# A second mixture in 11 column tiles: the third tile in strips that a count gives out, its weights copied by ScalarE, and a ring of 13 wide tiles in the first mixture

## The chip, the core and the metric

The kernel runs on one core of a Trainium2 chip. TensorE is called PE here, VectorE DVE, ScalarE ACT, GpSimd POOL and SyncE SP. The metric is the device time of one launch in microseconds (us): 2194.33 us, the median of three runs (2190.61 to 2199.8). The execution that the profiler recorded took 2192.68 us.

## The reference, cut to what matters

Two transformer blocks run one after the other on 256 tokens of 1024 features, in float32. Both have a mixture of experts; all else (attention, time mixing, dense products, norms) is not touched by the change but for a few places of buffers.

```python
def expert_block(args):              # first mixture: 32 experts, hidden 512, two experts for a token
    xb, e = args
    return (jax.nn.silu(xb @ w_gate[e]) * (xb @ w_up[e])) @ w_down[e]
...
def moe_swiglu(x, router_w, router_b, w1, w3, w2):   # second mixture: 8 experts, hidden 2816
    logits = (x @ router_w + router_b).astype(jnp.float32)
    top_v, top_i = lax.top_k(logits, TOP_K)          # TOP_K = 2
    top_p = jax.nn.softmax(top_v, axis=-1)
    gate = jnp.sum(jax.nn.one_hot(top_i, N_EXPERTS_2, dtype=jnp.float32) * top_p[..., None], axis=-2)
    out = jnp.zeros_like(x)
    for e in range(N_EXPERTS_2):
        out = out + gate[..., e:e + 1] * swiglu(x, w1[e], w3[e], w2[e])
    return out
```

With 256 tokens and two experts for each, an expert of the first mixture gets 16 tokens in the mean, one of the second 64. With the inputs of the runs no expert of the first mixture has more than 30; those of the second have 81, 47, 76, 46 and 65, 81, 65, 51.

## The kernel before

The program is a list of phases, run in order: `b1` (first block's mixer), `moe1` (first mixture), `mix0`, `ffn0`, `ple0`, `mix1`, `ffn1` (the second mixture, function `moe2`), `ple1`, `fin`. Weights come from memory as tiles of 1 MB (128x2048) that SP loads, in the order in which they are used, into a ring of places; a load is issued as soon as the tile that had its place before is released. A phase can widen the ring: `WIDE` gives the number of places that it adds, 9 in `moe1` (12 with the three of the base) and 6 in `ffn1`.

A mixture routes tokens by matrix products. A one-hot matrix `P` (tokens by slots) is made on DVE from the place of each token in its expert's list (`At`, `places`, `pos`); PE gathers the tokens of the slots with it (`gathered`, into `xg`); the experts' products are computed for slots; and the results are combined back with the transposed and weighted matrix (`pw`, `pt`). If an expert has more tokens than slots, a branch (`overflow`, an If on all engines, on the flag `fi` that DVE makes) computes the rest; with these inputs the branch's body is not run, but its test is.

**First mixture.** 32 experts with 32 slots each, 8 groups `g` of four experts. A group takes 16 tiles `wgu` (first products) and 8 tiles `wdn` (down). The test of the overflow stands after group 3.

**Second mixture.** The 8 experts are two halves `c` of four. For each half there are 11 blocks `j` of first products, each of 8 tiles `w<-m` (`k`, a slice of 128 of the 1024 features; four experts side by side, 512 columns each), then two down products `d` of 22 tiles each: 264 tiles in all. Each expert has `CAP2` = 96 slots, so that a half has 384 slots, which are three PSUM banks of 128. The function `tiles` does one tile: 12 matmuls, each of 32 slots (the stationary side) by 512 columns of the slots' expert, each on a quarter (32 columns) of the array. Four quarters make one bank, so a tile is three rounds of four.

After the 8 tiles of a block `j`, ACT does Silu on each bank's gate half (`ft`, 128x256) and DVE multiplies by the other half; DVE transposes the result in pieces into `hT`, the input of the down product. At the end of a down product (below called a d-end) ACT takes each bank with a scale to `yh` (128x512), DVE takes what rounding left to `yl`, and PE combines both into the tokens with `pt`. The banks are double: the next block can use three others meanwhile. The overflow's test stands at `c` = 1, `j` = 5. In `route_in` the input is split in a high and a low part (`htmh`, `html`); of four low parts two are made on DVE and two on POOL.

Instructions go to each engine's queue in program order, but for work put in `beside` or `later`, which is laid between the tiles. All queues run in order.

Of the kernel before, what the change touches and what calls it, by code (L numbers as in the profile page):

```python
# [119 lines left out]
def prep(I):  # L120
# [88 lines left out]
    g, u = [I[n][0].reshape(2, 4, 8, 128, 11, 256).transpose(0, 4, 2, 3, 1, 5) for n in ("moe_w1_2", "moe_w3_2")]  # L209
    A["m13"] = np.concatenate([g, u], -1)  # L210
# [65 lines left out]
class Kern:  # L276
# [275 lines left out]
    def run(self):  # L552
        tc, nc, A = self.tc, self.nc, self.A
        with ExitStack() as ctx:
# [4 lines left out]
            self.wsp = pool("wsp", SPLIT)  # L559
# [27 lines left out]
            self.room, wider = ExitStack(), set()  # L587
# [6 lines left out]
            for i, ph in enumerate(self.phases):  # L594
                l = int(ph[-1]) if ph[-1].isdigit() else 0
                if ph == "ple0":
                    other = split(second.enter_context(tc.tile_pool(reuse_waits="tile", name="raw", bufs=1)))
                new = (self.phases + [""])[i + 1]
                self.ends = new == "fin"
# [18 lines left out]
                if ph == "mix1":  # L618
                    second.close()
            if self.phases[-1] != "fin":  # L620
                nc.sync.dma_start(self.out.rearrange("k p s -> p k s"), x)
# [16 lines left out]
    def block1(self, x, early):  # L638

        tc, nc = self.tc, self.nc  # L640
        with ExitStack() as late, ExitStack() as ctx:
# [6 lines left out]
            nc.gpsimd.dma_start(a2, self.A["a2"])  # L648
            h = [pool.tile([128, 8, S], F32R, name="h" + c) for c in "hl"]
# [41 lines left out]
            out = late.enter_context(tc.tile_pool(reuse_waits="tile", name="b1o", bufs=1, side="right"))  # L691
            mg = out.tile([128, 8, S], F32, name="mg")
            mh = out.tile([128, 8, S], F32R, name="mh")
            ml = out.tile([128, 8, S], F32R, name="ml")
# [231 lines left out]
    def places(self, pool, oh1, oh2, n, beside):  # L926
# [6 lines left out]
        for t in range(2):  # L933
            o = b.t[:, n * t:n * t + n]
            b.mm(o, self.cst("triu"), At[:, t])
            if t:
                b.mm(o, self.cst("ones"), At[:, 0])
        with self.after((nc.cur_bb, added)):
# [3 lines left out]
        nc.vector.scalar_tensor_tensor(ps, pv, 1.0, At, op0=ALU.add, op1=ALU.mult)  # L942
        return ps
# [19 lines left out]
    def overflow(self, pool, x, xs, rs, wo, fi, n, units, w13, w2):  # L963
# [3 lines left out]
        tc, nc = self.tc, self.nc  # L967
        wT = pool.tile([32, S], F32, name="wT")
        ec = pool.tile([32, 2], F32, name="ec")
        rv = nc.values_load(fi, min_val=0, max_val=1, skip_runtime_bounds_check_because="made by a comparison")  # L970
        with tc.If(rv != 0, preferred_fallthrough_block=False):  # L971
# [10 lines left out]
            for k in range(8):  # L982
                nc.vector.tensor_mul(xs[:, k], xs[:, k], b.t[:, :S])
# [4 lines left out]
            def unit(i, e):  # L988
                nc.vector.scalar_tensor_tensor(ec[:, 1:2], ec[:, 0:1], float(e), self.cst("pidx")[:32],
                                               op0=ALU.add, op1=ALU.is_equal)  # L990
                sel = self.wsp.tile([128, 512], F32, name="wh")
# [1068 lines left out]
```

## Time and the profile before

| | |
|---|---|
| time, median of three runs | 2194.33 us (2190.61 to 2199.8) |
| profiled execution | 2192.68 us, of which the recorded span is 2191.1 us |
| PE busy | 2047.4 us, 93% of the span |
| DVE, ACT, POOL busy | 48%, 29%, 1% |
| memory traffic | 613.44 MB, 280 GB/s in the mean |
| first mixture, its products | about 345 to 800 us |
| second mixture, its products | about 1420 to 2142 us |

The span is cut into stages by the tiles that are loaded. A busy share of a whole span says little here: in one stretch PE waits for loads, in another loads wait for PE. So the stages are read apart, by what stood in the windows and by which engine's wait ends last.

### The profile page before, as it was taken

To read this page: it belongs to the slowest core of one execution; us is meant where nothing else is said; L and a number is where in the kernel's file an instruction comes from. 1 tells how busy PE (TensorE), PEld (TensorE's weight loads), DVE (VectorE), ACT (ScalarE), POOL (GpSimd) and SP (SyncE) were. 2 spreads that over 40 slices of the span, in tenths; PEclk is the share of its full clock that TensorE was granted. 3 is DMA by queue.
4 is the path that set the end of the run, shared out by engine and by line. 5 is a ranking of instruction groups with operands and counts; after the bars stand their busy time and mean duration, and the time that the engine had idled before them with its cause. 6 is when DMAs were issued, how large, how long until landed. Compare 5 with 4: busy or idle time off the path is not lost. (4 is left out here: it accounts for less than half of the span.)

```text
span 2191.1 us, 39956 instructions
## 1 busy us (share of the span) xinstructions
PE 2047.4 (93%) x16640; PEld 1241.8 (57%) x16640; DVE 1061.6 (48%) x2770; ACT 629.9 (29%) x1298; POOL 23.7 (1%) x33
## 2 busy tenths in 40 slices
PE   7999998787787779999999999999999999999997
PEld 6999995222222238889999988842222333233336
DVE  5787654010000028677666777636554006555105
ACT  5466642000000025365556735410000000001005
POOL 0000000000000010000000100000000000000000
PEclk9999999999999999999999999899999999999999
DMA  5344586999999983315555341479999999999972
GB/s 177 118 145 138 174 343 260 420 419 420 418 420 420 420 363 117 119 59 200 190 192 189 113 138 40 173 264 384 410 407 409 388 377 402 400 363 408 409 306 91
DMA packets 88640, 613.44 MB, mean 280 GB/s; under 512 B 9879, under 2 KB 12071, under 8 KB 18560
## 3 DMA queue, kind: packets, MB, share of 16 engines
q1 hardware_dynamic: 86272, 604.74, 70.8%
q0 software_dynamic: 1344, 5.10, 0.7%
q8 instruction: 133, 2.18, 0.4%
q10 hardware_dynamic: 832, 0.94, 0.1%
q14 instruction: 59, 0.48, 0.1%
HBM read 609.69 MB, written 1.05 MB: 279 GB/s over the span
## 5 line engine op out<-in xcount | busy, mean ns | idle before, releaser
L228 PE MATMUL ps<-w,xg 128*32 128x512 f32 x2432 | 428.9, 600 | 54.9 <-DMA w<-wgu 48.2
L340 DVE TENSOR_TENSOR wl<-w,wh 128x512 fp32r<-128x512 f32 (+2 forms) x500 | 318.9, 652 | 169.4 <-ACT wh L339 158.5
L339 ACT CAST wh<-w 128x512 fp32r<-128x512 f32 (+2 forms) x500 | 289.6, 585 | 296.1 <-PE ps L228 254.6
L228 PE MATMUL ps<-w,hT 128*32 128x512 f32 x2624 | 338.3, 593 | 30.3 <-DMA w<-wdn 24.9
L228 PEld LDWEIGHTS ps<-w,xg 128*32 128x32 f32 x2432 | 97.9, 110 | 306.0 <-issue 180.7
L228 PE MATMUL ps<-rawh,wh 128*128 128x256 f32 x896 | 258.9, 289 | 0.0
L1989 DVE STREAM_TRANSPOSE hT<-ft 32x64 f32<-32x64 f32 x1056 | 249.2, 236 | 17.7 <-DVEq L971 0.7
L228 PE MATMUL ps<-rawh,wl 128*128 128x256 f32 x896 | 252.5, 282 | 1.5 <-DVE rawl L353 1.5
L228 PE MATMUL ps<-rawl,wh 128*128 128x256 f32 x896 | 252.3, 282 | 0.0
L228 PEld LDWEIGHTS ps<-w,hT 128*32 128x32 f32 x2624 | 91.2, 110 | 264.6 <-issue 189.7
L228 PE MATMUL ps<-w,rawl 128*32 128x512 f32 x1408 | 201.9, 597 | 5.2 <-DVE hT L1989 5.2
L228 PEld LDWEIGHTS ps<-rawh,wh 128*128 128x128 f32 x896 | 169.6, 189 | 3.8 <-issue 1.4
L228 PEld LDWEIGHTS ps<-rawh,wl 128*128 128x128 f32 x896 | 169.7, 189 | 3.5 <-DVE rawl L353 1.7
L228 PEld LDWEIGHTS ps<-rawl,wh 128*128 128x128 f32 x896 | 169.5, 189 | 1.1 <-DVE ast L1789 0.2
L228 PE MATMUL ps<-w,rawh 128*32 128x512 f32 x1408 | 167.9, 595 | 0.0
L301 ACT ACTIVATE ft<-ps,rsl 128x256 f32<-128x256 f32 x66 | 31.3, 474 | 415.8 <-PE ps L228 415.8
L228 PE MATMUL ps<-hh,wh 128*128 128x256 f32 x416 | 125.8, 303 | 0.0
L228 PEld LDWEIGHTS ps<-w,rawl 128*32 128x32 f32 x1408 | 56.5, 111 | 110.7 <-issue 108.9
L228 PE MATMUL ps<-hh,wl 128*128 128x256 f32 x416 | 117.4, 284 | 0.1
L228 PE MATMUL ps<-hl,wh 128*128 128x256 f32 x416 | 117.3, 282 | 0.0
L1981 DVE SCALAR_TENSOR_TENSOR ft<-ps,rsl,ft 128x256 f32<-128x256 f32 x66 | 31.9, 484 | 168.5 <-ACT ft L301 167.1
L1204 DVE SCALAR_TENSOR_TENSOR sg<-ps,rsl,sg 128x512 f32<-128x512 f32 x8 | 6.0, 749 | 209.1 <-PE ps L228 175.8
(492 smaller groups left out, 2708.8 us busy)
## 6 DMA issues: line engine op xcount, KB each, us to landing
w<-m SPq DMA_DIRECT2D x264, 1024.0 KB, 7.3
w<-wgu SPq DMA_DIRECT2D x128, 1024.0 KB, 19.9
w<-wdn SPq DMA_DIRECT2D x64, 1024.0 KB, 19.9
w<-f SPq DMA_DIRECT2D x32, 1024.0 KB, 4.9
w<-wz SPq DMA_DIRECT2D x20, 1024.0 KB, 5.0
w<-wdh SPq DMA_DIRECT2D x24, 768.0 KB, 4.3
w<-wb SPq DMA_DIRECT2D x16, 1024.0 KB, 5.1
w<-wo SPq DMA_DIRECT2D x8, 1024.0 KB, 5.3
```

What stands on the lines that cost most here:

```text
L228: return self.k.nc.tensor.matmul(out, lhsT, rhs, start=new, stop=stop, skip_group_check=True, **kw)
L301: r = sc.activation(out, in_, func, **kw)
L339: self.nc.scalar.copy(h, src)
L340: self.nc.vector.tensor_sub(l, src, h.bitcast(F32))
L1204: nc.vector.scalar_tensor_tensor(sg, acc[1].t, rsl[:, g:g + 1], sg, op0=ALU.mult, op1=ALU.mult)
L1981: nc.vector.scalar_tensor_tensor(t, g[r].t[:, 256:], u, t, op0=ALU.mult, op1=ALU.mult)
L1989: nc.vector.transpose(hT[f:f + 32, 2 * j:2 * j + 2, 128 * r + s:128 * r + s + 32], ts[r].rearrange("p (i d) -> p i d", i=2)[s:s + 32, :, f ...
```

## The change

Four parts of it move work.

**The second mixture's slots.** `CAP2` falls from 96 to 64, so that two banks hold the four experts' 64 slots. The third bank holds 3 strips of 32 slots, which go to three of the four experts: all but the one with the fewest tokens (`fewest` makes a mask `mk` from the counts that `places` now gives, and the experts' numbers `ei`; `strips` and `more` make the strips' columns of `P`). A strip's 512 columns are put on the four quarters in pieces: `parts` lists six matmuls of 384, 128, 256, 384, 256 and 128 columns, 384 on each quarter. Which expert's weights a strip needs is known only at run time, so ACT copies the strip's 128x512 from the tile into a buffer `fw` (two of them, `FLEX`) with an address from a register: three copies for a tile, 792 in all. As the strip's pieces lie at several places of the third bank, its evictions go in pieces too: three of 128x64 in place of one Silu of 128x256, and at a d-end 12 of 32x128 into `yfh` and `yfl` in place of one of 128x512. `pt`, `wsl`, `rsl` have five rows for a half in place of three.

**The first mixture.** The ring has 13 more places in place of 9. The one-hot matrix is made for each pair of groups, when it is needed.

**The input's split.** All four low parts are made on DVE; POOL and its two raw copies are gone.

**The overflow.** `keep_input` is gone (the branch makes its input itself), and the test moves to group 0 of the first mixture, and to `c` = 0, `j` = 5 of the second.

```diff
-WIDE = {"b1": 0, "moe1": 9, "mix0": 0, "mix1": 0, "ffn0": 2, "ffn1": 6, "ple0": 4, "ple1": 4, "fin": 0}
+WIDE = {"b1": 0, "moe1": 13, "mix0": 0, "mix1": 0, "ffn0": 2, "ffn1": 6, "ple0": 4, "ple1": 4, "fin": 0}
...
-CAP1, CAP2 = 32, 96
+CAP1, CAP2 = 32, 64
+
+FLEX = 2
...
             nc.scalar.copy(hi, b.t)
-            if not k0:
-                return lambda: nc.vector.tensor_sub(lo, b.t, hi.bitcast(F32))
-            raw = self.tmp.tile([128, 512], F32, name="mt")
-            nc.scalar.copy(raw, b.t)
-            nc.gpsimd.tensor_sub(lo, raw, hi.bitcast(F32))
+            return lambda: nc.vector.tensor_sub(lo, b.t, hi.bitcast(F32))
...
-            def tiles(banks, lhs, w):
-                for u in range(12):
-                    r, c = divmod(u, 4)
-                    l, o = [v for v in lhs if v[1] <= 32 * u][-1]
-                    banks[r].mm(banks[r].t[32 * c:32 * c + 32], l[:, 32 * u - o:32 * u - o + 32], w[:, u // 3],
-                                q=(c, c + 1), tile_position=(0, 32 * c))
...
+        parts = ((0, 0, 0, 0, 384), (1, 0, 0, 384, 512), (2, 0, 1, 256, 512), (3, 0, 2, 128, 512),
+                 (1, 128, 1, 0, 256), (2, 256, 2, 0, 128))
...
+            def tiles(banks, lhs, w, c):
+                for u in range(8):
+                    r, q = divmod(u, 4)
+                    banks[r].mm(banks[r].t[32 * q:32 * q + 32], lhs[0][:, 32 * u:32 * u + 32], w[:, u // 2],
+                                q=(q, q + 1), tile_position=(0, 32 * q))
+                fw = pool.tile([128, 3, 512], F32, name="fw", bufs=FLEX)
+                for f in range(3):
+                    self.cp(fw[:, f:f + 1], w[:, bass.ds(who[c][f], 1)])
+                for q, o, f, a, b in parts:
+                    banks[2].mm(banks[2].t[32 * q:32 * q + 32, o:o + b - a], lhs[1][:, 32 * f:32 * f + 32],
+                                fw[:, f, a:b], q=(q, q + 1), tile_position=(0, 32 * q))
...
+                who += [[nc.values_load(ei[:, c, i:i + 1], engines=(mybir.EngineType.Activation,), min_val=0, max_val=3,
+                                        skip_runtime_bounds_check_because="made by a comparison") for i in range(3)]
+                        for c in range(2)]
...
-                            self.act(t, g[r].t[:, :256], AF.Silu, scale=u)
-                            nc.vector.scalar_tensor_tensor(t, g[r].t[:, 256:], u, t, op0=ALU.mult, op1=ALU.mult)
...
+                            for q, u in [(slice(0, 4), r)] if r < 2 else [(slice(b, b + 1), 2 + of_block[b]) for b in range(3)]:
+                                u = rsl[:, 5 * c + u:5 * c + u + 1]
+                                self.act(t4[:, q], gu[:, q, 0], AF.Silu, scale=u)
+                                nc.vector.scalar_tensor_tensor(t4[:, q], gu[:, q, 1], u, t4[:, q], op0=ALU.mult, op1=ALU.mult)
...
-                            yh, yl = [work.tile([128, 512], F32R, name="y" + n, bufs=3) for n in "hl"]
...
+                            for p, a, e, o, u in pieces:
+                                yh, yl = [y[p, o:o + e - a] for y in ys[r]]
+                                sc = wsl[p, 5 * c + u:5 * c + u + 1]
+                                self.act(yh, g[r].t[p, a:e], AF.Copy, scale=sc)
+                                nc.vector.scalar_tensor_tensor(yl, g[r].t[p, a:e], sc, yh.bitcast(F32), op0=ALU.mult, op1=ALU.subtract)
```

The change writes a few orders anew. Three places follow. In each row a line, an operation and its operands stand, and what the instruction waits for (a semaphore of an engine or a DMA queue); x3 is three in a row. A matmul's right-hand names are the moving side and the stationary side.

On PE, in a down product of the second mixture, one tile was this before (the wait is for the tile's load):

```order
L228 MATMUL ps<-w,hT 32x512 [waits DMAHW1_49]
L228 MATMUL ps<-w,hT 32x512 x11
L228 MATMUL ps<-w,hT 32x512 [waits DMAHW2_49]
L228 MATMUL ps<-w,hT 32x512 x11
L228 MATMUL ps<-w,hT 32x512 [waits DMAHW3_49]
```

and is this now:

```order
L230 MATMUL ps<-w,hT 32x512 [waits DMAHW1_49]
L230 MATMUL ps<-w,hT 32x512 x7
L230 MATMUL ps<-fw,hT 32x384 [waits Activation_49]
L230 MATMUL ps<-fw,hT 32x128
L230 MATMUL ps<-fw,hT 32x256 [waits Activation_49]
L230 MATMUL ps<-fw,hT 32x384 [waits Activation_49]
L230 MATMUL ps<-fw,hT 32x256
L230 MATMUL ps<-fw,hT 32x128
```

Four of the 12 matmuls are replaced by six shorter ones, and three of these wait for ACT's copies.

On ACT, in the first products of the second mixture, nothing stood between the Silus of two blocks before (29 in a row here, then the three evictions of each of two d-ends):

```order
L301 ACTIVATE ft<-ps,rsl 128x256 [waits PE_49] x4
L301 ACTIVATE ft<-ps,rsl 128x256 [waits DVE_49,PE_49] x29
L299 ACTIVATE yh<-ps,wsl 128x512 [waits PE_49] x3
L299 ACTIVATE yh<-ps,wsl 128x512 [waits DVE_49,PE_49] x3
L301 ACTIVATE ft<-ps,rsl 128x256 [waits PE_49] x4
```

Now, from the last tile of one block into the first of the next (ISA sets a register for the copy behind it):

```order
L314 COPY fw<-w 128x512
L303 ACTIVATE ft<-ps,rsl 128x256 [waits PE_49]
L314 ISA
L314 COPY fw<-w 128x512
L303 ACTIVATE ft<-ps,rsl 128x256 [waits DVE_49,PE_49]
L303 ACTIVATE ft<-ps,rsl 128x64 [waits DVE_49,PE_49]
L314 ISA
L314 COPY fw<-w 128x512 [waits DMAHW3_49,Activation_49]
...
L303 ACTIVATE ft<-ps,rsl 128x64 [waits DVE_49]
L314 ISA
L314 COPY fw<-w 128x512
L303 ACTIVATE ft<-ps,rsl 128x64 [waits DVE_49]
```

The third copy of the old block's last tile stands behind the first Silu, and the pieces of the third bank, each behind DVE's piece before it, stand between the copies of the next block's first tile.

On ACT, at the last d-end, with the next phase's casts (`wh`, `ph`) around it, before:

```order
L299 ACTIVATE yh<-ps,wsl 128x512 [waits PE_49,Activation_49]
L339 CAST wh<-w 128x512 [waits DMASW5_49,DMASW4_49,DMASW6_49,DMASW3_49,DMASW7_49,DMASW2_49,DMAHW2_49,DMASW1_49,DMASW0_49]
L299 ACTIVATE yh<-ps,wsl 128x512 [waits PE_49,Activation_49]
L339 CAST wh<-w 128x512 [waits DMASW4_49,DMASW0_49]
L299 ACTIVATE yh<-ps,wsl 128x512 [waits PE_49,Activation_49]
L339 CAST wh<-w 128x512 [waits DMAHW3_49,DMASW7_49,DMASW3_49]
L339 CAST wh<-w 128x512 [waits DMASW6_49,DMASW2_49]
```

and now:

```order
L301 ACTIVATE yh<-ps,wsl 128x512 [waits PE_49] x2
L341 CAST wh<-w 128x512 [waits DMAHW2_49]
L301 ACTIVATE yfh<-ps,wsl 32x128 [waits PE_49]
L341 CAST wh<-w 128x512
L341 CAST wh<-w 128x512 [waits DMAHW3_49]
L301 ACTIVATE yfh<-ps,wsl 32x128 [waits DVE_49]
L341 CAST wh<-w 128x512
L301 ACTIVATE yfh<-ps,wsl 32x128 [waits DVE_49] x10
L301 ACTIVATE mt<-x 128x512 [waits DVE_49]
```

One eviction has become 12, and 11 of them wait for DVE. Behind them on PE stand the matmuls with `pt` that combine, and only behind these the next phase's products (`ph`, `pl`), which stood between them before.

## Rows read from the trace of the kernel before

**Rows 1.** The page: PE's busy share, and the traffic in 40 slices.

```profile
PE 2047.4 (93%) x16640; PEld 1241.8 (57%) x16640; DVE 1061.6 (48%) x2770; ACT 629.9 (29%) x1298; POOL 23.7 (1%) x33
...
GB/s 177 118 145 138 174 343 260 420 419 420 418 420 420 420 363 117 119 59 200 190 192 189 113 138 40 173 264 384 410 407 409 388 377 402 400 363 408 409 306 91
```

**Rows 2.** Windows of the first mixture: length, busy (instructions) by engine, clock, DMA share, GB/s.

```profile
310.00:320.00 10.00, 10.00 (x86) 10.00 (x86) 5.95 (x9) 5.45 (x10) 0.00 (x0) 1.00 1.01 421
320.00:330.00 10.00, 10.00 (x88) 10.00 (x88) 2.09 (x4) 1.10 (x2) 0.00 (x0) 1.00 0.52 186
330.00:340.00 10.00, 5.88 (x41) 5.48 (x40) 7.93 (x34) 4.42 (x10) 2.48 (x2) 0.82 0.00 0
340.00:350.00 10.00, 7.88 (x50) 4.61 (x50) 5.34 (x24) 0.68 (x2) 0.00 (x0) 0.67 0.11 20
...
400.00:800.00 400.00, 311.71 (x1462) 85.22 (x1460) 29.88 (x45) 18.79 (x30) 1.43 (x3) 0.99 1.01 419
```

**Rows 3.** PE's waits in 400 to 800 us: released by, us, times, longest.

```profile
PE ps L228 <- DMA w<-wgu: 47.0, 74, 1.6
...
PE ps L228 <- issue: 6.5, 1, 6.5
```

**Rows 4.** Windows of the second mixture, columns as in rows 2.

```profile
1460.00:1664.00 204.00, 204.00 (x1908) 61.03 (x1904) 126.75 (x508) 13.04 (x28) 0.00 (x0) 1.00 1.00 399
1664.00:1784.00 120.00, 120.00 (x1107) 38.51 (x1100) 18.61 (x59) 5.55 (x9) 0.00 (x0) 1.00 0.98 396
```

**Rows 5.** Waits of SP's queue in 1450 to 2140, and of PE in 1460 to 2140.

```profile
SPq L262 <- PE ps L228: 581.3, 224, 9.7
...
PE ps L228 <- DVE hT L1989: 5.2, 1, 5.2
```

**Rows 6.** Timeline at one block's end: start, us, engine, what; in brackets the idle time before.

```profile
1559.94 1.90 PE L228 MATMUL ps<-w,rawh 128*32 128x512 f32 x16
...
1561.07 0.47 ACT L301 ACTIVATE ft<-ps,rsl 128x256 f32<-128x256 f32 x1 [18.41 <-PE ps L228]
...
1561.93 0.47 ACT L301 ACTIVATE ft<-ps,rsl 128x256 f32<-128x256 f32 x1 [0.39 <-PE ps L228]
...
1562.52 1.90 PE L228 MATMUL ps<-w,rawh 128*32 128x512 f32 x16
```

**Rows 7.** Timeline of PE, in the second half's first products.

```profile
1895.82 0.59 PE L228 MATMUL ps<-w,xg 128*32 128x512 f32 x1
1896.22 0.61 PE L228 MATMUL ps<-w,rawl 128*32 128x512 f32 x3
```

**Rows 8.** Timeline of ACT: four casts of 128x512 in a row.

```profile
14.44 2.18 ACT L339 CAST wh<-w 128x512 fp32r<-128x512 f32 x4 [1.22 <-DMA w<-wgv]
```

**Rows 9.** Timeline of the second mixture's routing.

```profile
1411.71 0.17 DVE L915 TENSOR_REDUCE t2n<-t2o 128x2 f32<-128x16 f32 x1
1411.80 2.49 POOL L1046 TENSOR_TENSOR html<-mt,htmh 128x512 fp32r<-128x512 f32 x2 [71.03 <-DVE t2o L914]
1411.91 1.19 DVE L916 TENSOR_TENSOR t2o<-t2o,t2n 128x16 f32<-128x16 f32 x1
...
1413.13 1.20 DVE L931 TENSOR_TENSOR At<-t1o,t2o 128x16 f32<-128x16 f32 x1
1414.25 1.28 DVE L1043 TENSOR_TENSOR html<-ps,htmh 128x512 fp32r<-128x512 f32 x2
...
1415.67 1.03 DVE L1910 TENSOR_TENSOR P<-pos,c 128x384 fp32r<-128x384 f32 x2
...
1419.68 0.36 ACT L299 ACTIVATE xg<-ps,pv 128x128 f32<-128x128 f32 x1
...
1420.99 0.34 DVE L1065 TENSOR_SCALAR xg<-ps,pv 128x128 f32<-128x128 f32 x1
```

**Rows 10.** Timeline behind the last down product.

```profile
2142.11 0.70 ACT L299 ACTIVATE yh<-ps,wsl 128x512 fp32r<-128x512 f32 x1
...
2143.18 0.74 DVE L2011 SCALAR_TENSOR_TENSOR yl<-ps,wsl,yh 128x512 fp32r<-128x512 f32 x1
```

More of the change, by code (lines that the diff above doesn't have):

```diff
@@ L596, in run @@
                 if ph == "ple0":
-                    other = split(second.enter_context(tc.tile_pool(reuse_waits="tile", name="raw", bufs=1)))
+                    extra = second.enter_context(tc.tile_pool(reuse_waits="tile", name="raw", bufs=1))
+                    extra.tile([128, 16], F32, name="pad")
+                    other = split(extra)
                 new = (self.phases + [""])[i + 1]
+                if ph in ROUTED:
+                    cuts.close()
+                elif not i or self.phases[i - 1] in ROUTED:
+                    parted("right" if ph == "b1" else "left")
                 self.ends = new == "fin"
@@ L690, in block1 @@
             early()
[L691 to L694, printed above, removed]
+            mg, (mh, ml) = gates[:, 0:8], self.parts
             self.dense_fm(og, lambda n, p: nc.vector.tensor_mul(mg[:, n:n + 2], p, gates[:, n:n + 2]),
@@ L961, in shares, with overflow @@
         return Wt
[L963 removed]
+    def overflow(self, pool, x, xs, rs, wo, fi, n, units, w13, w2, of13=None):
         tc, nc = self.tc, self.nc
+        keep, xs, back = xs
         wT = pool.tile([32, S], F32, name="wT")
@@ L1181, in experts1 @@
             next(start)
+            for do in subs:
+                do()
             for g in range(8):
@@ new lines, in strips @@
+                def strips(src, name):
+                    s, o = four(src), rt.tile([128, 2, 2, 3, 4], F32, name=name)
+                    d = rt.tile([128, 2, 2, 3], F32, name=name + "d")
+                    nc.vector.tensor_sub(d, s[:, :, :, 1:4], s[:, :, :, 0:3])
+                    nc.vector.tensor_tensor(d, d, mk[:, None].to_broadcast([128, 2, 2, 3]), op=ALU.mult)
+                    nc.vector.tensor_add(d, d, s[:, :, :, 0:3])
+                    for i in range(3):
+                        n = 3 - i
+                        nc.vector.tensor_copy(o[:, :, :, i, :n], d[:, :, :, :n])
+                        nc.vector.tensor_copy(o[:, :, :, i, n:], d[:, :, :, n - 1:])
+                    return o.rearrange("p t c i g -> p t c (i g)")
@@ L1913, in gather, with more @@
+                def more(c):
+                    for t in range(2):
+                        nc.vector.tensor_tensor(v3(P[:, t, L * c + B:L * c + L], 32), bc(psx[:, t, c], 32),
+                                                iota[:, None, CAP2:CAP2 + 32].to_broadcast([128, 12, 32]), op=ALU.is_equal)
                 def gather(c):
-                    return self.gathered(xg[c], htm, P[:, :, R * c:R * c + R], "g_ffn1")
+                    return self.gathered(xg[c], htm, P[:, :, L * c:L * c + R], "g_ffn1")
@@ L1942, in moe2 @@
                 next(start)
+                for do in subs[2:]:
+                    do()
                 def during(k):
```

239 lines of the change are left out of this document (151 added, 88 removed).

## The prediction

> **What bounds the kernel now.** The page comes first: PE is busy 93% of the span, and the traffic stands at 417 to 420 GB/s in a run of slices in the first half and just under 410 in many of the second [rows 1]. So each mixture is read by its own windows and waits.
>
> In the first mixture, from 400 to 800 us, PE is busy 311.71 of 400 us while the DMA share is 1.01 at 419 GB/s; PE waits 47 us for `wgu` tiles alone [rows 2, 3]. Loads bound it. A tile of 1.0486 MB takes 1.0486/0.419 = 2.50 us. Ahead of it there is a hole: at 310 to 320 traffic is 421 GB/s, then 186, 0 and 20 in the next three windows of 10 us [rows 2]. The ring of 12 is full, routing isn't done, and nothing has been released. Of these 30 us the loads use 4.4 + 0 + 0.5, so about 25 us stand empty.
>
> In the second mixture it is the other way round: PE is busy 204 of 204 and 120 of 120 us at full clock [rows 4], SP's queue waits 581 us for PE to release tiles, and PE's one wait is 5.2 us, at the overflow's test [rows 5]. PE bounds it, though not by much: traffic is at 399 and 396 GB/s. A step (one tile) takes 1562.52 - 1559.94 = 2.58 us [rows 6]; three banks end 0.86 us apart (1561.07, 1561.93). Ten blocks of 8 steps are 206 us, which the 204 us window shows.
>
> **The ring of 13.** Four more tiles are loaded in the hole: 4 x 2.50 = -10.0 us, as behind it the loads run without a gap and end the stage. The test at group 0 is hidden as it was at group 3: PE's one wait of 6.5 us [rows 3] falls where the DMA share stays 1.01 over the whole window. If group 0's ring ran full during the test, it would give back up to 6.5.
>
> **POOL's part removed.** Two small DVE operations take 1.19 and 1.20 us while POOL's two subtractions run, where one of the same kind takes 0.17 [rows 9]. That chain leads to `At`, for which PE waits. Removing POOL is worth (1.19 - 0.17) + (1.20 - 0.17) = 2.05 us. The first mixture has the same pair at its own routing (POOL busy 2.48 in 330 to 340 [rows 2]); its releases, and so all its loads, start 2 us sooner: -2.0. The Trainium skill (SBUF — State Buffer, Terms) says that DVE and GpSimd share a port pair, exclusively, and that the loser is blocked for a whole instruction; the rows agree, two DVE operations each waiting about a POOL one.
>
> **The second mixture's start.** After `pos`, DVE does about 23 small operations (`cn`, `fewest`, `strips`, parts of the shares) at 0.17 us, and four makings of `P`, against two of 384 columns before (1.03 us for both [rows 9]): about 3.9 + 1.8 - 1.0 = +4.7. Two low parts move from POOL to DVE at 0.64 each: +1.3. Less POOL's 2.05, and with some 0.4 saved on 352 instead of 384 gathered columns: +3.5 us. ACT's three loads of an expert's number have no row alone; they lie below 5.2 us (the whole test of rows 5, which has one and a branch) and beside the gather, so I take nothing, and 0 to 5 for the range.
>
> **A step.** The third round of a tile falls from 512 to 384 columns on each quarter: 0.86 x 384/512 = 0.64 us, and the step to 0.86 + 0.86 + 0.64 = 2.36, if unequal pieces on the four quarters pack. One view bears on this: at 1895.82 one matmul of the next product (`xg`) runs alone and three of the following one start 0.40 us later [rows 7], so quarters do not move in lockstep. The Trainium skill (TensorEngine Tiling (Array Packing), Key Properties) says that tiles of the array load and multiply independently of each other; by it too the step is 2.36.
>
> **The copies.** Four casts of 128x512 in a row take 2.18 us on ACT, 0.55 each [rows 8]. An address from a register and the ISA ahead of it have no row. Three copies are 1.64 us, below 2.36, so in a steady stretch they hide behind PE. Bounds: 0.55 (nothing added) to about 0.9 (the 0.55 and again the 0.36 that a small ACT operation costs [rows 9]); I take 0.6. The traffic doesn't change.
>
> **A block's end.** What isn't hidden is here. Take the end of bank 0 as zero. ACT's Silu starts at 0.27 (the round that begins at 1559.94 is over 0.86 later, at 1560.80, and the Silu starts at 1561.07 [rows 6]) and holds ACT to 0.74; the third copy of the old block's last tile stands behind it and ends at about 1.3. PE wants it at 0.86: 0.5 us lost on one quarter. Bank 2 then ends at 1.97; Silu's piece starts at 2.24, two copies follow, the next piece, then the third copy of the next block's first tile, at about 4.4; PE wants it at 3.7: 0.7 lost. After that two buffers of `fw` suffice. So a block costs 8 x 2.36 + 1.2 = 20.1 to 20.3 us instead of 20.6. The loads need 8 x 2.50 = 20.0, so they nearly end it too. 21 blocks: 21 x -0.4 = -8.4.
>
> **The down products.** 88 tiles x (2.36 - 2.575) = -18.9. At each d-end 12 pieces go to and fro between ACT (0.36) and DVE (0.34) [rows 9] with some 0.05 of signalling: 0.75 each, 9 us, and the next tiles' copies stand between them on ACT. The first two tiles lose about 0.8 and 0.7 us, and the combining matmuls, put into the third, wait for the last pieces at about 11.5 us, when PE would have come there by 10 to 11: 2 us a d-end, three of them: +6.
>
> **The last d-end** has no further tile to hide it. Before, the third bank's `yh` starts at 2142.11 and its `yl` ends at 2143.92 [rows 10], 1.8 us. Now 12 pieces of 0.75 are 9 us, with casts between the first: about +7.5; PE's products of the next phase now stand behind them in its queue, and PE, idle for so long, may start again at the lower of its two levels (1.2 instead of 2.4 GHz), as the mean of 0.67 at 340 to 350, behind the routing's idle time, shows for a part of that window [rows 2]. I take +9 (7 to 12).
>
> **Sum.** 2192.7 - 12.0 + 3.5 - 8.4 - 18.9 + 6 + 9 = 2171.9 for the profiled execution; the median of before lies 1.65 us above that, so 2174. What else the diff moves (buffers shared in `b1`, pads, the combine's operands) leaves order and counts as they were: nothing, within 3 us.
>
> **Rivals.**
>
> *The boundaries cost twice* (no change or a little slower). If a copy takes 0.75, and pieces with their signals near 0.9, a block's end loses 2.6 instead of 1.3 and a d-end 5 instead of 2, the last one 2 more: +27 + 9 + 2 = 2212. Halfway it is 2193. For it: four small chains that each wait across two engines; against: with 0.24 us of evictions a step besides the copies' 1.8, ACT has half a microsecond to spare in each step and runs ahead. 0.26.
>
> *ACT becomes the bound* (slower). With evictions (about 0.24 us a step) ACT's step is 3 copies + 0.24; it passes the old 2.58 from 0.78 us a copy. At 0.9 it is 2.94: +0.36 x 256 = 92 above before's, less 12 and plus 12.5: 2287; at 0.8 about 2210. Against it: the 0.55 of a cast, 0.23 short of that [rows 8]. 0.09.
>
> *The pieces don't pack* (slower). If a second wave waits for all quarters, the third round is 0.64 + 0.43 = 1.07 and the step 2.79: +0.215 x 256 = 55, so about 2192.7 - 12 + 55 + 15 = 2251. The quarters out of step speak against it [rows 7]. 0.06.
>
> *The boundaries hide* (faster still). If copies run well ahead, 21 x 1.3 + 6 = 33 us come back: 2140. The loads set a floor: from 1460 us [rows 4] to the last eviction at 2142 [rows 10] are some 681 us, in which 21 x 8 + 88 = 256 tiles, less 9 that the ring already holds, take 617 us at 2.50: a gain of 64 at most, so they wouldn't stop it. 0.14.
>
> **Chances and range.** My forecast, 0.45, lies at 2160 to 2190, its part below 2183 the larger. A measurement of this kernel tells about 0.5% (11 us) from no change, so faster is below 2183.4: 0.37 of the forecast, 0.14 of the hidden boundaries, and 0.09 of the costly ones: 0.60. Within 0.5%: 0.08 + 0.13 = 0.21. Slower, above 2205: 0.04 + 0.09 + 0.06 = 0.19. The range leaves out half of the hidden boundaries below 2142, and above 2216 most of the last two slow cases and a rest: 2142 to 2216.
>
> **What the changed profile would show.** The hole in the first mixture about 10 us shorter, its end some 12 us earlier. In the second mixture's windows matmul groups `ps<-fw` whose step is 2.36; PE waits released by ACT `fw`, twice for each block, about 1.2 us in sum, some 25 us in all; SP's waits for PE much shorter. The groups of `fw` copies at 0.55 to 0.65 us each. At the end an idle PE of about 7 us with ACT `yfh` and DVE `yfl` in turn. Wrong I would be by a copy above 0.75 us, by a third round of over 0.9 us, or if loads fell below 400 GB/s in the second mixture, which would then end each block.

## The result, and the profile after

The changed kernel takes 2168.49 us (four runs, 2165.67 to 2169.89) against 2193.87 us of before beside it: 0.9884 of before, 95% interval 0.987 to 0.9898, so 25 us or 1.16% faster. The forecast was 2174, within 2142 to 2216. The profiled execution took 2167.51 us, its span is 2165.9.

The page after, with the lines that answer to [rows 1], the group of the new copies, and the loads of the second mixture (issues, KB each, us to landing: 7.3 before):

```profile
PE 2016.7 (93%) x17740; PEld 1461.7 (67%) x17740; DVE 1060.6 (49%) x2809; ACT 1080.2 (50%) x2178; POOL 18.7 (1%) x29
...
GB/s 179 120 146 149 175 376 305 418 420 420 419 420 420 419 343 109 109 61 216 179 193 191 114 128 52 175 159 396 399 410 418 416 405 407 418 418 417 418 351 47
...
L314 ACT COPY fw<-w 128x512 f32 x792 | 439.0, 617 | 137.3 <-ACT fw L314 91.9
...
w<-m SPq DMA_DIRECT2D x264, 1024.0 KB, 10.7
```

PE is as busy as before, in a shorter span; ACT went from 29% to 50%. In the second mixture's slices traffic now stands at 396 to 418 GB/s, where it was 363 to 410.

Windows of the profile after; columns as in [rows 2]:

```profile
310.00:320.00 10.00, 10.00 (x89) 10.00 (x88) 4.12 (x8) 3.68 (x7) 0.00 (x0) 1.00 1.01 419
320.00:330.00 10.00, 10.00 (x83) 10.00 (x83) 2.71 (x11) 2.90 (x6) 0.00 (x0) 0.91 0.99 410
330.00:340.00 10.00, 3.82 (x17) 3.35 (x16) 8.40 (x37) 1.48 (x4) 0.00 (x0) 0.67 0.03 13
...
1390.00:1400.00 10.00, 10.00 (x50) 10.00 (x49) 2.42 (x12) 2.27 (x6) 0.00 (x0) 0.50 0.84 338
1425.00:1430.00 5.00, 5.00 (x35) 3.30 (x28) 0.71 (x2) 2.15 (x6) 0.00 (x0) 0.77 0.43 141
1440.00:1445.00 5.00, 5.00 (x34) 2.48 (x38) 0.17 (x1) 0.52 (x2) 0.00 (x0) 0.66 0.28 115
1460.00:1550.00 90.00, 90.00 (x1069) 58.66 (x1065) 60.08 (x244) 68.44 (x137) 0.00 (x0) 1.00 0.99 397
1580.00:2040.00 460.00, 459.30 (x5207) 311.37 (x5202) 205.98 (x816) 340.92 (x662) 0.00 (x0) 1.00 1.01 415
```

The hole in the first mixture's loads [rows 2] is filled in 320 to 330: 410 GB/s where there were 186. Three windows ahead of and in the second mixture's first block have a mean clock of 0.50, 0.77 and 0.66: PE ran at the lower level (1.2 GHz) for all or part of them. And from 1580 to 2040 us, loads run at 415 GB/s with a DMA share of 1.01, nearly the 419 of the first mixture.

PE's waits in 1440 to 2125 us (us, times, longest), which answer to [rows 5]:

```profile
PE ps L230 <- ACT yfh L301: 7.0, 2, 6.6
PE ps L230 <- issue: 6.4, 1, 6.4
PE ps L230 <- ACT fw L314: 0.3, 2, 0.2
```

6.6 us stand at the last d-end, 6.4 at the overflow's test; the copies show as 0.3 us only. One quarter of the array that waits while the others work is no idle PE, so what the copies cost doesn't stand in this view; it is read from the distance of two blocks.

The timeline after: PE's steps in a down product and behind the one-column products of the routing, and ACT at two blocks' ends and at the last d-end:

```profile
1421.22 2.29 PE L230 MATMUL ps<-rs,P 128*128 128x1 f32 x20
1423.44 3.24 PE L230 MATMUL ps<-w,rawh 128*32 128x512 f32 x16
...
1495.29 0.47 ACT L303 ACTIVATE ft<-ps,rsl 128x256 f32<-128x256 f32 x1
...
1514.22 0.47 ACT L303 ACTIVATE ft<-ps,rsl 128x256 f32<-128x256 f32 x1
...
1598.97 0.47 ACT L303 ACTIVATE ft<-ps,rsl 128x256 f32<-128x256 f32 x1 [1.48 <-PE ps L230]
...
1600.51 0.32 ACT L303 ACTIVATE ft<-ps,rsl 128x64 f32<-128x64 f32 x1 [0.20 <-PE ps L230]
1600.72 0.61 ACT L314 COPY fw<-w 128x512 f32 x1
1601.23 0.32 ACT L303 ACTIVATE ft<-ps,rsl 128x64 f32<-128x64 f32 x1
1601.44 1.13 ACT L314 COPY fw<-w 128x512 f32 x2
...
1618.52 0.48 ACT L303 ACTIVATE ft<-ps,rsl 128x256 f32<-128x256 f32 x1 [1.48 <-PE ps L230]
...
2101.55 1.95 PE L230 MATMUL ps<-w,hT 128*32 128x512 f32 x16
...
2103.91 1.96 PE L230 MATMUL ps<-w,hT 128*32 128x512 f32 x16
...
2111.08 0.36 ACT L301 ACTIVATE yfh<-ps,wsl 32x128 fp32r<-32x128 f32 x1 [0.61 <-DVE yfl L2125]
2111.86 0.36 ACT L301 ACTIVATE yfh<-ps,wsl 32x128 fp32r<-32x128 f32 x1 [0.41 <-DVE yfl L2125]
```

A step is 2103.91 - 2101.55 = 2.36 us, as forecast. A block takes 1514.22 - 1495.29 = 18.93 us in the first half's early part and 1618.52 - 1598.97 = 19.55 later, where it took 20.60. The pieces at the last d-end follow each other at 0.78 us.

Cut by the same instructions in both traces, the difference of the spans (25.2 us) goes so:

| stretch, between starts of instructions | before, us | after, us | change | forecast |
|---|---|---|---|---|
| start to the first product with the first router's weights (`sm`) | 319.9 | 315.2 | -4.7 | 0 |
| to the last multiplication of group 7 in the first mixture (`sg`) | 465.6 | 454.9 | -10.7 | -12 |
| to the last product with the second router's weights | 622.3 | 626.8 | +4.5 | 0 |
| to the second mixture's first gathering matmul | 8.6 | 12.4 | +3.8 | +3.5 |
| to the first Silu (the first block) | 41.7 | 49.3 | +7.6 | 0 |
| to the last Silu (21 blocks, two down products, a test) | 563.1 | 535.8 | -27.3 | -21.3 |
| to the last down matmul | 119.7 | 111.8 | -7.9 | (in the row above) |
| to the end | 50.1 | 59.7 | +9.6 | +9 |

### The profile page after: what moved, and what is told of

It reads as the page before. It is cut to its first block, busy times and chain, and to the rows that moved or that the text cites. A ratio compares the mean times of both kernels' runs of the same rounds, so it can differ in the third digit from the quotient of the medians.

```text
span 2165.9 us, 44126 instructions
## 1 busy us (share of the span) xinstructions
PE 2016.7 (93%) x17740; PEld 1461.7 (67%) x17740; DVE 1060.6 (49%) x2809; ACT 1080.2 (50%) x2178; POOL 18.7 (1%) x29
## 5 line engine op out<-in xcount | busy, mean ns | idle before, releaser
L314 ACT COPY fw<-w 128x512 f32 x792 | 439.0, 617 | 137.3 <-ACT fw L314 91.9
L230 PE MATMUL ps<-w,hT 128*32 128x512 f32 x1920 | 311.0, 597 | 31.4 <-DMA w<-wdn 26.0
L230 PE MATMUL ps<-fw,xg 128*32 128x384 f32 (+2 forms) x2112 | 252.8, 382 | 0.0
L230 PE MATMUL ps<-w,xg 128*32 128x512 f32 x1024 | 199.5, 600 | 43.2 <-DMA w<-wgu 43.0
L230 PE MATMUL ps<-w,rawh 128*32 128x512 f32 x1408 | 206.2, 607 | 6.4 <-issue 6.4
L230 PEld LDWEIGHTS ps<-w,hT 128*32 128x32 f32 x1920 | 116.8, 110 | 135.6 <-DMA w<-wdn 64.0
L230 PEld LDWEIGHTS ps<-fw,xg 128*32 128x32 f32 x2112 | 137.8, 110 | 83.0 <-issue 24.0
L230 PEld LDWEIGHTS ps<-w,xg 128*32 128x32 f32 x1024 | 42.1, 109 | 185.7 <-DMA w<-wgu 111.7
L230 PEld LDWEIGHTS ps<-w,rawl 128*32 128x32 f32 x1408 | 105.2, 110 | 34.4 <-issue 0.9
L230 PE MATMUL ps<-fw,hT 128*32 128x128 f32 (+2 forms) x1056 | 121.1, 380 | 0.5 <-ACT fw L314 0.3
## 6 DMA issues: line engine op xcount, KB each, us to landing
w<-m SPq DMA_DIRECT2D x264, 1024.0 KB, 10.7
```

The source lines that it names most:

```text
L230: return self.k.nc.tensor.matmul(out, lhsT, rhs, start=new, stop=stop, skip_group_check=True, **kw)
L314: self.nc.scalar.copy(out, in_)
```

## The experiments

**The kernel before once more**, and **the changed one without its pads**. The first mixer's 4.7 us were in no one's sum. The second edit is this, at four places:

```diff
-            pool.tile([128, 16], F32, name="pad")
...
-            T("pad", (128, 16))
```

Expected of the first:

> The kernel before, unchanged, profiled once more. The profile after has the first mixer (b1) ending 4.9 us sooner than before, at a steady drift of some 0.016 us for each us, though its orders are the same. Theory A (the drift belongs to the changed kernel: buffers lie elsewhere): the first matmul with the router's weights is again at about 319.8 us, and 315 in the profile after. Theory B (it is how one execution differs from the next): this run lies 2 us or more away from 319.8, nearer to 315.

Expected of the second:

> The changed kernel without its four small pads (64 or 32 bytes a partition), which move the buffers behind them. Theory A (the pads are what makes the first mixer 4.9 us shorter): the first matmul with the router's weights goes from 315.0 back to about 319.8 us, and the spacing of the matmuls of 128x256 from 0.113 to 0.12. Rival (another shared or moved buffer, or chance): it stays within 1 us of 315.

Measured, by the products with the routers' weights in the view of the tile `sm` (durations in ns, then the first and the last start). The kernel before, once more:

```profile
L228 PE MATMUL ps<-sm,x x64: 256/279/361, 319.9 to 1407.8; 128*128 128x36 f32 x32, 128*128 128x8 f32 x32
```

The changed kernel:

```profile
L230 PE MATMUL ps<-sm,x x64: 256/279/363, 315.2 to 1396.9; 128*128 128x36 f32 x32, 128*128 128x8 f32 x32
```

Without pads:

```profile
L230 PE MATMUL ps<-sm,x x64: 256/268/279, 320.0 to 1394.4; 128*128 128x36 f32 x32, 128*128 128x8 f32 x32
```

Before repeats its 319.9 to a tenth, and without pads the changed kernel is back at 320.0. In all eleven profiled executions with pads this product starts at 312.9 to 315.2. So the pads make the first mixer 4.8 us shorter, theory A in both; why buffers 32 or 64 bytes further on help its matmuls stays open. PE's mean granted clock up to 312 us is 0.98 without pads and 0.99 with them in the changed kernel, so the clock may be a part of it. Yet without pads the whole took 2165.39 us in its one run, not more: from the last `sg` to the last `sm` product it needed 619.6 us, where before needs 622.3. With pads this stretch, whose orders are the same in all versions but the two with wide sums below, took 623.2 to 627.7 us in nine executions (the changed kernel and eight experiments that alter nothing there). Its windows without pads, in the changed kernel, and in the run with nine wide places that follows, each with 5619 matmuls:

```profile
774.80:1394.40 619.60, 605.41 (x5619) 549.39 (x5620) 429.45 (x874) 324.51 (x688) 14.54 (x17) 0.99 0.42 146
770.10:1396.90 626.80, 611.89 (x5619) 555.50 (x5620) 429.66 (x874) 324.68 (x688) 14.58 (x17) 0.98 0.42 147
780.40:1408.10 627.70, 613.95 (x5619) 556.69 (x5619) 429.88 (x874) 324.47 (x688) 14.55 (x17) 0.97 0.41 144
```

The time goes with PE's mean granted clock: 622.3 us and 0.99 in the kernel before, 627.6 or 627.7 us and 0.97 in four of the nine executions with pads. The clock falls at other places from one execution to the next with nothing changed there, so this stretch doesn't show that the pads cost anything; one execution without them can't tell whether they move the clock. A single run tells a gain of 3 to 5 us only by the stretch in which it lies.

**Nine wide places** in the first mixture:

```diff
-WIDE = {"b1": 0, "moe1": 13,
+WIDE = {"b1": 0, "moe1": 9,
```

Expected:

> The changed kernel with 9 wide places in the first mixture again in place of 13. Theory A (four tiles more in the hole ahead of the first mixture): the last tile of the first mixture ends 4 x 2.50 = 10 us later than in the profile after, and the time is about 2178. Rival (the 14 us that the first mixture ends sooner come from the routing and from what lies ahead, loads being late elsewhere): the end moves by under 4 us and the time stays at 2168 to 2172.

Measured: 2176.24 us, 0.9915 of before (0.9899 to 0.9932). From the first `sm` product at 314.0 to the last `sg` at 780.4 it takes 466.4 us; with 13, from 315.2 to 770.1, 454.9. The ring alone is worth 11.5 us there, a little above 4 x 2.50, and the stretch with 9 is no shorter than before's 465.6: all else that changed in the first mixture, POOL's removal among it, gave nothing. Theory A holds. (A ring of 13 in the kernel before wasn't run.)

**The last third bank in one piece:**

```diff
-                            pieces = [(slice(0, 128), 0, 512, 0, r)]
-                            if r == 2:
+                            pieces = [(slice(0, 128), 0, 384 if r == 2 else 512, 0, r)]
+                            if r == 2 and (c, d) != (1, 1):
```

Expected:

> The changed kernel with the third bank of the last down product evicted in one piece of 128x384 on each of the two engines, where 12 pieces of 32x128 stood. The strips then get one strip's scale and lie in the wrong columns, so it computes something else at that place; all else is the same. Theory A (the 12 pieces going to and fro are what the last end lost: 9.5 us from the last matmul of the down product to the end, against before): the time falls by 7 to 9 us, to about 2160. Rival (the end is longer since the next phase's products stand behind the combining matmuls in PE's queue): it falls by under 4.

Measured: 2155.24 us in one run. From the last down matmul to the end it takes 51.6 us in place of 59.7; before had 50.1. The whole is 12 us below the changed kernel's profiled execution; 3.5 of the rest lie ahead of the second routing (623.3 us for 626.8), where nothing differs. The row of ACT:

```profile
2102.86 0.58 ACT L301 ACTIVATE yfh<-ps,wsl 128x384 fp32r<-128x384 f32 x1
```

The 12 pieces cost 8.1 us at the end. Theory A.

**Four tiles for the pieces:**

```diff
-                yf = [work.tile([128, 512], F32R, name="yf" + n) for n in "hl"]
+                yf = [[work.tile([128, 128], F32R, name=f"yf{n}{o}") for o in range(4)] for n in "hl"]
...
```

Expected:

> The changed kernel with yfh and yfl as four tiles of 128x128 each (one for each 128 output columns) in place of one of 128x512. Neighbouring pieces then lie in different tiles, so ACT's piece no longer waits until DVE has read the piece before it. Theory A (the 9 us are the waiting to and fro, 0.75 for each pair): ACT and DVE run side by side, 12 pieces in 4 to 5 us, the tail from the last down matmul to the end falls from 59.7 to about 55, each of the other three ends of a down product gains 1 to 2, and the time is about 2160. Rival (a piece costs what it costs, and the wait is only where the time shows): the tail stays within 1 us of 59.7.

Measured: 2166.88 us, 0.9879 of before (0.9862 to 0.9895), no different from the changed kernel; the tail is 59.6. The pieces still wait, in the timeline:

```profile
2109.71 0.36 ACT L301 ACTIVATE yfh<-ps,wsl 32x128 fp32r<-32x128 f32 x1 [0.41 <-DVE yfl L2125]
2110.48 0.36 ACT L301 ACTIVATE yfh<-ps,wsl 32x128 fp32r<-32x128 f32 x1 [0.41 <-DVE yfl L2125]
```

So the wait isn't for the tile that is written. What was left in common is the PSUM bank that both engines read.

**The third bank copied first**, then taken to pieces from the copy (with four tiles as above):

```diff
+                            src = g[r].t
+                            if r == 2:
+                                src = self.tmp.tile([128, 512], F32, name="mt")
+                                self.cp(src[:, :384], g[r].t[:, :384])
...
-                                self.act(yh, g[r].t[p, a:e], AF.Copy, scale=sc)
+                                self.act(yh, src[p, a:e], AF.Copy, scale=sc)
```

Expected:

> The changed kernel with the third bank of a down product first copied from PSUM in one piece (128x384, ACT), the 12 pieces then taken from that copy, into four tiles each. With four tiles alone ACT's piece still waited for DVE's, both reading the one PSUM bank. Theory A (the order of two engines on one PSUM bank makes the to and fro): read from the copy, ACT's pieces follow each other at about 0.27 us, DVE's a step behind, all 12 in about 4 us instead of 9.3, and the tail goes from 59.7 to about 55. Rival (pieces alternate anyway, by the tiles that they write or the scales that they read): the tail stays at 59 or above, one copy longer.

Measured: 2166.24 us in one run; the tail is 56.9 us. ACT and DVE now run side by side:

```profile
2109.37 3.98 ACT L301 ACTIVATE yfh<-mt,wsl 32x128 fp32r<-32x128 f32 x12
...
2110.12 3.62 DVE L2129 SCALAR_TENSOR_TENSOR yfl<-mt,wsl,yfh 32x128 fp32r<-32x128 f32 x12
```

12 pieces in 4 us: theory A on the cause. The time hardly moved, as the tail gained 2.8 and not 4.7, and the last inner d-end gave the same back: from the first `yh` of one to that of the next it is 63.3 us (2043.2 to 2106.5), where the changed kernel has 60.8 (2044.3 to 2105.1). There the 12 pieces in one row hold up the next tiles' copies: none starts between 2045.07 and 2049.60, and PE waits 1.0 us for `fw`, where it waits 0.2 in the changed kernel.

**Wide columns.** The slots' scales and weights are products with one column on the moving side. Here it is 48 equal ones:

```diff
-                b.mm(b.t[:, r:r + 1], P[:, t, 128 * r:128 * r + 128].bitcast(F32), col[:, t:t + 1])
+                b.mm(b.t[:, 48 * r:48 * r + 48], P[:, t, 128 * r:128 * r + 128].bitcast(F32), col[:, t:t + 1].to_broadcast([128, 48]))
...
```

Expected:

> The changed kernel with the products of one column (slots' scales and weights, of_slots and the ones behind Pw) made 48 columns wide, all alike; the first is used. Theory A (behind the runs of 20 one-column matmuls PE's granted clock falls, and the next tile's 16 matmuls take 3.1 to 3.2 us where they take 1.9): the clock stays at the upper level, and the first block of the second mixture is about 2.9 us shorter, 46.4 instead of 49.3 us from the first gathering matmul to the first Silu. Rival (the first block's 7.5 us more are the number of matmuls added, and the clock falls in any case): it stays within 1 us of 49.3, or gets longer as each matmul does more.

Measured: 2160.52 us, 0.9853 of before (0.9831 to 0.9874). From the first gathering matmul (1404.2) to the first Silu (1450.9) it is 46.7 us. Windows of the first block:

```profile
1420.00:1425.00 5.00, 5.00 (x48) 3.52 (x44) 1.24 (x4) 2.87 (x7) 0.00 (x0) 1.00 0.60 185
1425.00:1430.00 5.00, 5.00 (x49) 3.01 (x44) 0.89 (x3) 2.64 (x7) 0.00 (x0) 1.00 0.58 202
...
1435.00:1440.00 5.00, 5.00 (x52) 3.04 (x55) 0.68 (x3) 2.06 (x5) 0.00 (x0) 1.00 0.30 79
```

From 1415 us to the block's end the clock stays at 1.00, and 2.6 us of the block's 7.6 come back. Theory A: the same stretch takes 49.0 to 50.0 us in all nine executions with narrow columns, and 45.7 to 46.7 in the three with wide ones. The other 5 agree with the added matmuls (40 for scales where there were 24, 40 for weights where there were 24, 20 transposes where there were 12): to the start of the next matmul these take 11.8 us in sum here, and 6.9 in the kernel before. Of the 8 us by which the time fell only the 2.6 are shown to be this edit's; 3.6 more lie, between the profiled executions, ahead of the second routing, where it changes nothing.

**Wide sums too.** The sums of squares ahead of both routings, 64 columns wide in place of one:

```diff
-                b.mm(b.t[:, t:t + 1], sq[:, i, ts], ones[:, 0:1])
+                b.mm(b.t[:, 64 * t:64 * t + 64], sq[:, i, ts], ones[:, 0:64])
...
```

Expected:

> The changed kernel with wide one-column products as in the run before, and the sums of squares ahead of both routings (one column behind each square) 64 columns wide as well. Theory A (runs of matmuls with one to eight columns are what lets PE's granted clock fall): the windows ahead of the second routing, 0.50 to 0.8 in other runs, stay at 1.0, the stretch from the last product of the mixer to the tokens' transposes gets 3 us shorter, and the time is 2157 to 2160. Rival (the logits' products of eight columns, which stay, let it fall as well, or the fall is due to something else): the clock falls there as before, and the time is that of the run with wide columns, 2160.5, or above as the sums do more work.

Measured: 2157.09 us, 0.9826 of before (0.9791 to 0.9861). The window ahead of the routing, with wide columns alone:

```profile
1380.00:1390.00 10.00, 10.00 (x76) 9.88 (x74) 2.70 (x4) 1.95 (x4) 0.00 (x0) 0.83 0.24 84
```

With wide sums:

```profile
1380.00:1390.00 10.00, 10.00 (x89) 9.88 (x88) 2.08 (x3) 2.52 (x4) 0.00 (x0) 1.00 0.29 102
```

The clock stays up here, as theory A has it; the time agrees with it, but the interval holds the rival's 2160.5 as well. And the run without pads, whose sums are narrow, keeps the clock too, from its first to its last product with the second router's weights:

```profile
1384.90:1394.40 9.50, 9.50 (x86) 9.50 (x86) 1.83 (x3) 1.89 (x3) 0.00 (x0) 1.00 0.24 81
```

These products span 9.5 us with wide sums, in both executions that have them. With narrow sums they span 11.1 us in eight of twelve executions, 14.3 to 14.5 in three (the changed kernel's among them, at a mean clock of 0.64), and 9.5 in this one. So the lower clock costs 1.6 to 5 us here; that wide sums keep it up is likely, but not shown.

**One Silu for the third bank:**

```diff
-if r < 2 else [(slice(b, b + 1), 2 + of_block[b]) for b in range(3)]
+if r < 2 else [(slice(0, 3), 2)]
```

Expected:

> The changed kernel with one Silu and one multiplication for the third bank (128x192 in one) in place of three each; the strips get one strip's scale, so it computes something else there. Theory A (ACT's and DVE's pieces between the copies are what a block loses at its end): the blocks behind the overflow's test take 18.9 us in place of 19.55, 16 of them 10 us less. Rival (loads: 8 tiles at 417 GB/s are 20 us, so PE goes at their pace): they stay at 19.5.

**The overflow's test late** (`c == 1 and j == 5`). Expected:

> The changed kernel with the overflow's test of the second mixture at the sixth block of the second half again. In the profile after, the five blocks ahead of the test take 18.93 us and all behind it 19.55. Theory A (behind the test the queues start anew, and ACT's copies stand otherwise against the Silus): blocks take 18.93 up to the test wherever it stands, so ten blocks of the first half do, and those behind it 19.55; the time falls by about 6 us. Rival (the ring's head start is used up after some six blocks, and loads set the pace from there): the change of pace stays at the sixth or seventh block.

Measured: with one Silu, 2166.8 us in one run, and the later blocks take 19.45 us in place of 19.55 (Silus at 1599.53 and 1618.98). With the test late, 2170.57, and the first half's blocks take 17.71, three times 18.93, 18.72, 19.93, and 19.55 from there (Silus at 1592.16 and 1611.71), with no test near. Both theories A fall. The pace changes at the same block wherever the test stands, and the separate pieces cost only 0.1 of the 0.62 us.

**No copies:**

```diff
-                for f in range(3):
-                    self.cp(fw[:, f:f + 1], w[:, bass.ds(who[c][f], 1)])
...
-                                fw[:, f, a:b], q=(q, q + 1), tile_position=(0, 32 * q))
+                                w[:, f, a:b], q=(q, q + 1), tile_position=(0, 32 * q))
```

Expected:

> The changed kernel without ScalarE's copies: the strips' matmuls take the weights of experts 0 to 2 straight from the tile, so the choice of experts is left out. Theory A (the copies, standing behind the pieces of the third bank, are what costs 0.65 us a block behind the sixth and about 3 us at a d-end): all blocks take 18.9 us, and from the first Silu to the last down matmul it is some 15 us less than 647.6. Rival (loads set the pace there): blocks stay at 19.5, or PE's waits name `w<-m` and blocks go to 20, as 8 tiles at 417 GB/s take 20.1.

Measured: 2166.9 us in one run, no less than with copies. ACT's first Silus of six blocks near the end of the first products:

```profile
1887.65 0.48 ACT L303 ACTIVATE ft<-ps,rsl 128x256 f32<-128x256 f32 x1 [14.15 <-PE ps L230]
...
1906.59 0.48 ACT L303 ACTIVATE ft<-ps,rsl 128x256 f32<-128x256 f32 x1 [14.14 <-PE ps L230]
...
1925.67 0.47 ACT L303 ACTIVATE ft<-ps,rsl 128x256 f32<-128x256 f32 x1 [14.29 <-PE ps L230]
...
1946.96 0.47 ACT L303 ACTIVATE ft<-ps,rsl 128x256 f32<-128x256 f32 x1 [16.50 <-PE ps L230]
...
1967.13 0.47 ACT L303 ACTIVATE ft<-ps,rsl 128x256 f32<-128x256 f32 x1 [15.39 <-PE ps L230]
...
1987.08 0.47 ACT L303 ACTIVATE ft<-ps,rsl 128x256 f32<-128x256 f32 x1 [15.13 <-PE ps L230]
```

and what PE's weight loads wait for in 1930 to 2000 us there:

```profile
PEld ps L230 <- DMA w<-m: 5.6, 20, 1.2
```

Behind the first, and but for the one with the test, blocks take 18.93 us in both halves, those from the sixth on too, until the ring is empty; then 19.1, 21.3, 20.2 and 19.95, at the pace of the loads (8 x 2.50 = 20.0). From the first Silu (1459.3) to the last down matmul (2105.2) it is 645.9 us against 647.6. Both theories have a half: the copies do cost the 0.62 a block, and taking them away gains 1.7 us in the whole stage, since the loads end it then. What theory A says of the d-ends falls: from the first `yh` of one to that of the next it is 58.8 us in the first half and 60.8 in the second, and with copies 58.7 and 60.8.

**Wide columns, wide sums and the copied bank together.** Expected:

> The changed kernel with all that the experiments point to: wide columns, wide sums and the third bank's copy. The gains lie in three places that don't touch each other (first block of the second mixture 2.6, ahead of its routing up to 3, tail 5), so they should add: from 2168.5 to 2157, or 2155 if the sums help, 0.983 of before. Rival (a gain at one place is lost at the next, as loads then end later): 2162 or above.

Measured: 2153.01 us (2151.32 to 2155.92, five runs), 0.9811 of before (0.9784 to 0.9838), below both kernels. It lies under 2155, but its tail (56.9) and its last inner d-end (63.3 us) are those of the copied bank alone, so that part adds nothing net; against wide sums without it (0.9791 to 0.9861) the intervals overlap. The gain is the clock's: its mean over the profiled execution is 0.984, where the changed kernel has 0.976, and of the 14.5 us between the two, 9.8 lie ahead of the second routing (617.0 us for 626.8) and 3.1 in the first block. How much of the 9.8 the wide sums give, and how much is where the clock happened to fall, isn't shown: the run without pads took 619.6 there with narrow ones.

## Why the prediction was right, point by point

- **What bounds.** Loads in the first mixture and PE in the second were read rightly. That the second has small reserves over its loads was read, but not carried through: behind the change loads run at 415 GB/s from 1580 us on. They don't yet hold PE up there, as none of PE's waits above names a load, but they end the blocks as soon as the copies are gone. One sign that the prediction gave didn't come: SP's queue was to wait much less for PE, and from 1420 to 2125 us it waits 573.5 us, nearly as long as before (581.3 [rows 5]), with loads at almost their full rate. So a queue that waits for PE to release places isn't a sign of reserves. The rival of hidden boundaries said that the loads' floor of 617 us wouldn't stop it; the run without copies stopped at 645.9. The floor counted tiles only; at the start of the stage the ring is full and the loads wait for PE (397 GB/s in 1460 to 1550), and that time isn't made up. It is a part of the difference; the rest wasn't taken apart.
- **The ring of 13:** -10.0 forecast, 11.5 shown. The test at group 0 is hidden, as said.
- **POOL's removal:** the two slow DVE operations are gone, as the rows of before let expect [rows 9], but the first mixture's routing got hardly shorter and the second's longer. From the first product with the router's weights to `At` the first mixture takes 20.7 us, and took 21.0; in the second, from the last such product, it is 6.4 where it was 5.3: the two low parts that moved to DVE stand ahead of it. The term of -2.0 in the first mixture was wrong, the price of 2.05 against +1.3 in the second as well; the sum of that stretch, +3.8 against +3.5, was right by luck of its parts.
- **The first block:** forecast at nothing, measured +7.6. The added PE work (32 more matmuls with one column and 8 more transposes) has no term in the sum, and the clock's fall behind it, 2.6 us, wasn't seen.
- **A step:** 2.36 forecast and measured. The unequal pieces pack; the Trainium skill (TensorEngine Tiling (Array Packing), Key Properties) says that the array's tiles work independently of each other, and the trace agrees with the 2.36 us above.
- **The copies:** 0.6 taken. Two in a row take 1.13 us, so they start about 0.52 apart, with the register's address; the rival in which ACT becomes the bound is out.
- **A block's end:** the step that failed, though on the good side: 20.2 forecast, 18.93 and 19.55 measured, 25 us less over the 20 blocks without a down product ahead of them, where 8.4 were forecast for 21. The prediction lost 0.5 us a block to the third copy of the old block's last tile and 0.7 to that of the next block's first; the first of these isn't lost at all. The order of ACT was read one tile wrong. Counted through by three a tile, the copies around the first Silu in the rows of the change are those of the next block's first tile, not the old block's last: in these early blocks ACT copies a tile ahead of the Silus and nothing is lost (18.93 against 8 x 2.36 = 18.88). From the sixth block on, in this trace and in that with the late test, the Silus of the first two banks stand ahead of all the next tile's copies, and its three copies behind the first piece of the third bank. There the price can be read: the third bank ends 0.27 us ahead of its piece, at 1600.24; PE wants the next tile's third round 1.72 later, at 1601.96; the last copy ends at 1601.44 + 1.13 = 1602.57, 0.61 late, which is the 0.62 by which a block is longer.
- **The down products and d-ends:** from the first `yh` of one d-end to that of the next it is 58.7 us in the first half; 22 x 2.36 and before's 3.55 for combining leave 3.2 lost, where 2 were forecast. In the second half it is 60.8 where before took 63.7, and 1.8 is lost. The run without copies says that it isn't the copies that lose it; that it is the pieces isn't shown.
- **The last d-end:** +9 forecast, +9.6 measured, 8.1 of it by the pieces, as said. The cause of the to and fro is the bank, not the tile; the forecast only took it from the order.
- **Outside the sum:** the pads gave 4.8 us in the first mixer, which was taken as nothing, within 3; the stretch to the second routing took 4.5 more in the profiled run, 3.4 of it in the products with the router's weights (14.5 us at a mean clock of 0.64, where before took 11.1).

So the time came out 5.5 us under the forecast, by a block's end that was 17 us too dear, less the first block, the clock and the POOL term. The sum was better than its parts: in the table the stretches miss by 19 us in sum on the one side and 14 on the other, and that so little is left of it is luck.

## What to carry to other kernels

When one engine's step is shortened by a tenth, look at once who is next: here loads stood at 399 of 419 GB/s before, 5% from being the bound, and most of what the copies still cost at a block's end can't be had without faster loads (without copies the stage gains 1.7 us). Count an order through to its tile before pricing what "stands behind" what. Here 12 small evictions of one PSUM bank by two engines went to and fro; one copy out of the bank let both run, which paid at the last end, where no next work hides them (2.8 us), and cost nearly as much (2.5 us) where copies for the next tiles stood behind.

## What the runs showed of the hardware that wasn't expected

- Behind 20 one-column matmuls of the routing PE's granted clock fell: the next 16 matmuls took 3.24 us (at 1423.44) where others take 1.92, with windows of 0.77 and 0.66. With 48 columns in the same places the windows stay at 1.00, and the kernel is 8 us faster by its median, 2.6 of them in this block. Ahead of the second routing, behind one-column sums of squares, the clock fell in eleven of twelve executions, to different depths, and in neither of the two with sums 64 columns wide.
- Moving buffers by 32 or 64 bytes a partition changed the first mixer by 4.8 us, with the same orders; the cause is open.
- Copies with an address from a register, each with a register operation ahead, ran as close as plain casts did: two in 1.13 us, against four in 2.18 [rows 8].
